# Alternating halves for negated weight sums, deferred follow-up work, and a gate in halves, in a one-layer hybrid decoder kernel

## The chip, the cores and the metric

The kernel runs on one core of a Trainium2 chip. The metric is the device time of one launch in microseconds (us); lower is better. Three runs of the kernel before gave a median of 2035.74 us.

## The reference

One layer on x of shape (512 positions, 2048), float32. The parts that matter here:

```python
h = rms_norm(x, norm1_w)
proj = h @ w_in                       # q | k | v | z | x,B,C | dt
q, k, v, z, xbc, dt_raw = split(proj)
attn = moba_attention(rms_norm(q), rms_norm(k), v)     # 8 heads x 128
xbc = silu(causal_dwconv(xbc))                         # width 4
y = ssd_chunked_scan(xs, softplus(dt_raw + dt_bias), -exp(a_log), bm, cm) + d_skip * xs
y = rms_norm per group of 512 (y * silu(z))            # 2 groups
x = x + concat(attn, ssm) @ w_out
h = rms_norm(x, norm2_w)
u_gate, u_val = split(causal_dwconv(h @ w_up))         # width 3
return x + (silu(u_gate) * u_val) @ w_down
```

## The kernel before, in words

Every product is computed from float32 operands that are split in two: `hi` (a rounded copy, made by ScalarE) and `lo` (the rest, made by VectorE), and takes three matmuls: hi by hi, hi by lo, lo by hi. TensorE (PE) is fed from such splits all the time.

**Phase one** (lines up to about 1215) is the input projection, attention, the state-space part and the output projection. The weights arrive in chunks (`raw`, three buffers) and are used in *pieces*. A piece is 12 matmuls of 512 columns, or for the 16 pieces of the `wz` weights (k and dt, first pair of heads) 24 of 264 columns. The main loop (line 1197) runs once for each piece `i`. It queues, in this order: the loads of chunks ahead; the matmuls of piece `i` (`use`), which at the last piece of a projection call `done`; the steps of `presum(i)`; the split of piece `i+3` (`issue_split`, which has three `hi` and three `lo` buffers, so that the split of piece `i+3` waits until the matmuls of piece `i` have read theirs); from the output projection on, splits of the mixed heads (`split_mix`); and one round of `advance()`.

Pieces 0 to 15 are the first x columns, 16 to 23 the B and C columns of group 0, 24 to 39 `wz`, 40 to 47 the queries of heads 0 and 1, 48 to 63 keys and values of the next pair, 64 to 71 their queries, 72 to 87 z of group 1, 88 to 111 x, B, C of group 1, 112 to 159 the two pairs of heads left, 160 to 175 z of group 0, and from 176 on the output projection. In the trace a query piece reads `acc<-A,hi`, a keys-and-values piece `acc<-hi,A`.

All other work of phase one is written as Python generators (`g_conv`, `g_q`, `g_head`, `g_ssm`, `g_gate` and so on). `spawn` runs the first step of one and puts it in a list; `advance` runs further steps when a rough clock for each engine (`Paced`) says that the step's inputs are ready, or at the latest in the second round for an urgent one (the step `"soon"` makes one urgent). Every engine works through its own queue in the order in which instructions were written, so that an instruction that waits holds all that are queued behind it. `done` of a query, of a convolution and of the last convolution call `spawn` at once, and so their first step is queued ahead of `presum` and the split of piece `i+3`.

- `g_conv`: VectorE scales the projection into `u`, ScalarE starts the tap sum `t`, VectorE adds three taps.
- `g_q`: ScalarE writes `qh`, VectorE `ql`, ScalarE the square `t`; the second step sums `t` over the head on PE (`token_sums`, line 636), and a copy of the sums goes to `rows`.
- `g_gate(g)`: four times a multiplication by the gate (VectorE) and a square into `sz` (ScalarE), three additions of the squares, sums on PE, a power of -1/2, a broadcast through PE into `p`, and four multiplications by it. Only then is `ssm0` or `ssm1` set, which `split_mix` of any tile of that group waits for (it forces generator steps until the name is there).

**Sums of weights ahead of time.** Phase two uses a scheme with seven products in place of eight, which needs sums of weight blocks. `presum` makes some of them in DRAM during phase one. For the `q`-th block of the list `SUMMED`, counted by `o = i - 6 * q`: at 12 a block is loaded into `s1t` (two buffers); at 15, for the first eight (`MINUS`), ScalarE writes its negative into `minus` (line 1182; in the trace `Y<-s1t`); at 16 and 18 GpSimd starts DMAs that add a further block into `s1t` and into `minus` (lines 1184, 1186); at 21 both are saved by DMAs on SyncE's queue (lines 1189, 1192; `s3d<-Y`). `minus` is the upper half of the tile `Y[1]` (4 x 512 elements in each partition), which holds nothing until group 1 begins. As 21 of block q is 15 of block q+1, the save of one block is queued just ahead of the write of the next, into the same half. The eight writes come in pieces 15, 21, 27, 33, 39, 45, 51 and 57.

**Phase two** (from line 1217) is the up and down projections; nothing in it is changed.

Of the kernel before, what the change touches and what calls it, by code (L numbers as in the profile page):

```python
# [195 lines left out]
def body(ctx, tc, xT, wi, wz, wo, wu, wd0, wd1, wd2, pp, pf, outT, dbg={}):  # L196
# [93 lines left out]
    C = [cpool.tile([128, S], F32R if k > 3 else F32, name=f"C{k}") for k in range(NH)] + [None] * 8  # L290
    first_v = C[4:8]
    Y = [cpool.tile([128, 4, S], F32, name="Y%d" % g) for g in range(2)]
    minus = Y[1][:, 2:4, :].rearrange("p a b -> p (a b)")
    for k in range(4, 8):
        C[k] = None

# [72 lines left out]
    st = {}  # L369


    gens = []

    def spawn(g, urgent=False):
        step([g, 0.0, urgent, 0, 1])
# [206 lines left out]
    def g_gate(g, sz):  # L582

        while "y%d" % g not in st:
            yield
        say = None if g else "ready"
        for f in range(4):
            clk["last"] = ("pe", clk["pe"])
            V.tensor_tensor(C[8 + 4 * g + f], C[8 + 4 * g + f], sz[:, f, :], op=OP.mult)
            A_.activation(sz[:, f, :], C[8 + 4 * g + f], AF.Square)  # L590
            if f % 2:
                yield say
        for f in range(1, 4):
            V.tensor_tensor(sz[:, 0, :], sz[:, 0, :], sz[:, f, :], op=OP.add)
        yield say
        p = sm_tile()
        token_sums(p, sz[:, 0, :])
        rows = wk.tile([128, 128], F32, name="rows", bufs=2)
        V.tensor_copy(rows, p[:, :128])
        yield say  # L600
        p = sm_tile()
        T.transpose(p[:, :128], rows, identf)
        r = wk.tile([128, 4], F32, name="scq", bufs=3)
        V.tensor_scalar(r, p[:, 0:128:32], 1.0 / 512, EPS, op0=OP.mult, op1=OP.add)
        G.tensor_tensor(r, r, nhalf[:, 0:4], op=OP.pow)
        yield say
        p = sm_tile()
        for t in range(4):
            T.transpose(p[:, t * 128:(t + 1) * 128], r[:, t:t + 1].to_broadcast([128, 128]), identf)
        for f in range(4):  # L610
            y = C[8 + 4 * g + f]
            V.scalar_tensor_tensor(y, y, pc("sw", 4 * g + f), p, op0=OP.mult, op1=OP.mult)
        st["ssm%d" % g] = True


    def g_q(acc, hd):
# [227 lines left out]
    def add_fm(done):  # L844
        box = {}
        for h in range(2):
            add_chunk(next_src("fm"), 1024, [512, 512], fm_uses(XR, 8 * h, [4, 4], NK, box, done))

    def conv_done(g, kind, ci, fi=0):
        def done(acc):  # L850
            if g not in sgs:
                while "y0" not in st:
                    advance(True)
                sgs[g] = ssm_group(g)
            spawn(g_conv(acc, ci, sgs[g], kind, fi), True)
        return done

    def wide(done, srcs, R, pre=None, tok=False):
# [40 lines left out]
    def z_stage(g):  # L899

        box = {}

        def done(t, acc):
            if t == 0:
                while not g and "ssm1" not in st:
                    advance(True)
                box["sz"] = wk.tile([128, 4, S], F32, name="sz")
            sz = box["sz"][:, t, :]
            clk["last"] = ("pe", clk["pe"])
            V.tensor_tensor(sz, acc, rbc, op=OP.mult)  # L910
            A_.activation(sz, sz, AF.Silu)
            if t == 3:
                spawn(g_gate(g, box["sz"]), False if g else "ready")

        wide(done, lambda k: next_src("wide"), XR)
# [23 lines left out]
    def add_pair(p):  # L939
        pr = {}  # L940
        hds = [{"i": 2 * p + i, "pair": pr} for i in range(2)]

        def kv_done(t, acc):
            if t == 0:
                while p == 2 and ("head2" not in st or "head3" not in st):
                    advance(True)
                pr["v"] = v_home(p)
                pr["k"] = wk.tile([128, 4, 256], F32, name="kt")
                pr["ss"] = wk.tile([128, 4, 2], F32, name="rk", bufs=2)
            vh, vl = (x[t] for x in pr["v"])  # L950
            A_.activation(vh, acc[:, 256:], AF.Copy, scale=rstd[:, t:t + 1])
            V.tensor_copy(pr["k"][:, t, :], acc[:, :256])
            V.scalar_tensor_tensor(vl, acc[:, 256:], rstd[:, t:t + 1], vh.bitcast(F32),
                                   op0=OP.mult, op1=OP.subtract)
            if t == 3:
                spawn(g_keys(pr))
                for hd in hds:
                    spawn(g_head(hd))

        def kz_done(half):  # L960
            def done(t, acc):
                if half == 0:
                    if t == 0:
                        pr["v"] = v_home(p)
                        pr["k"] = wk.tile([128, 4, 256], F32, name="kt")
                        pr["ss"] = wk.tile([128, 4, 2], F32, name="rk", bufs=2)
                    V.scalar_tensor_tensor(dtr[:, t, :], acc[:, 248:264], rstd[:, t:t + 1], pc("dtb", 0, 16),
                                           op0=OP.mult, op1=OP.add)
                    V.tensor_copy(pr["k"][:, t, :248], acc[:, :248])
                    if t == 3:  # L970
                        spawn(g_dt())
                    return
                vh, vl = (x[t] for x in pr["v"])
                A_.activation(vh, acc[:, 8:264], AF.Copy, scale=rstd[:, t:t + 1])
                V.tensor_copy(pr["k"][:, t, 248:], acc[:, :8])
                V.scalar_tensor_tensor(vl, acc[:, 8:264], rstd[:, t:t + 1], vh.bitcast(F32),
                                       op0=OP.mult, op1=OP.subtract)
                if t == 3:
                    spawn(g_ssm(0, sgs[0]))
                    spawn(g_keys(pr))  # L980
                    for hd in hds:
                        spawn(g_head(hd))
            return done

        if p == 0:
            for half in range(2):
                box = {}
                for k in range(0, NK, 2):
                    add_chunk(next_src("kz"), 528, [528], [tok_use(k, 2, 264, box, kz_done(half))])
        else:  # L990
            wide(kv_done, lambda k: next_src("wide"), XR, tok=True)
        for hd in hds:
            add_fm(lambda acc, hd=hd: spawn(g_q(acc, hd)))

    add_pair(0)
    add_pair(1)
# [2 lines left out]
        add_fm(conv_done(1, "xs", 4 + i, i))  # L999
    add_fm(conv_done(1, "Bf", 9))  # L1000
    last_conv = conv_done(1, "Cf", 11)
    add_fm(lambda acc: (last_conv(acc), spawn(g_ssm(1, sgs[1]))))
    add_pair(2)
    add_pair(3)
    z_stage(0)
# [2 lines left out]
    def split_mix(i):  # L1008

        k = OK_ORDER[i]  # L1010
        name = "ssm%d" % ((k - 8) // 4) if k >= 8 else "head%d" % k
        while name not in st:
            advance(True)
        dump("mix%d" % k, C[k])
        A_.activation(A[i], C[k], AF.Copy)
        V.tensor_tensor(B[i], C[k], A[i].bitcast(F32), op=OP.subtract)
# [156 lines left out]
    def presum(i):  # L1173
        for q, g in enumerate(SUMMED):
            w = blocks[g][2].shape[-1]
            o = i - 6 * q
            if o == 12:
                s1t[g] = wk.tile([128, 1024], F32, name="s1t", bufs=2)
                nc.sync.dma_start(s1t[g][:, :w], blocks[g][2])
            elif o == 15 and g in MINUS:  # L1180
                s3t[g] = minus
                nc.scalar.activation(s3t[g][:, :w], s1t[g][:, :w], AF.Copy, scale=-1.0)
            elif o == 16:
                nc.gpsimd.dma_start(s1t[g][:, :w], blocks[g][3], accum_op=OP.add)
            elif o == 18 and g in s3t:
                nc.gpsimd.dma_start(s3t[g][:, :w], blocks[g][0], accum_op=OP.add)
            elif o == 21:
                s1d[g] = dram.tile([128, w], F32, name="s1d%d" % g)
                nc.sync.dma_start(s1d[g], s1t.pop(g)[:, :w])
                if g in s3t:  # L1190
                    s3d[g] = dram.tile([128, w], F32, name="s3d%d" % g)
                    nc.sync.dma_start(s3d[g], s3t.pop(g)[:, :w])
# [4 lines left out]
    for i, (ci, o, w, use) in enumerate(pieces):  # L1197
        issue_dma(ci + 3)
        clk["pe"] = max(clk["pe"], ready.get(i, 0.0))
        use(*his.pop(i))  # L1200
        presum(i)
        issue_split(i + 3)
        for j in mix_at.get(i - out_start, ()):
            split_mix(j)
        left = n_piece - i
        if left <= 8:
            issue_dma(n_raw + (8 - left) // 2)
        if left == 5:
            early_split("P1", raws[n_raw])
        if left == 2:  # L1210
            early_sum()
        advance()
# [453 lines left out]
```

## Time and profile before

| | |
|---|---|
| median of 3 runs | 2035.74 us (2035.19 to 2037.06) |
| the profiled execution | 2035.49 us |
| span in its profile | 2033.8 us |
| PE busy | 2018.0 us |
| VectorE (DVE) busy | 1561.2 us |
| ScalarE (ACT) busy | 1011.3 us |
| phase one ends at about | 770 us |

How to read it: the profile shows one execution. The span runs from the first to the last recorded instruction; 1.7 us of the launch lie outside it. In the view in order of time a row has its start, its length, engine, line, operation, the tile written and the tiles read, and the number of instructions put together; in square brackets stand the time that the engine sat idle before it and what it was waiting for. "L191" is the helper through which phase one issues its operations. PE rows of length 0.39 overlap with the next matmul, which starts earlier than that. SPq is SyncE's queue of DMAs.

### The profile page before, as it was taken

What the parts mean: (1) busy time and instruction counts of PE and PEld (TensorE: products, weight loads), DVE (VectorE), ACT (ScalarE), POOL (GpSimd) and SP (SyncE); (2) the same over time, 40 slices, a digit from 0 to 9 for tenths busy, and PEclk for the clock granted to TensorE, in tenths of its full rate; (3) what the DMA queues carried; (4) which work ended last, traced back from release to release, by engine and by line L of the source; (5) the groups of instructions that cost most, each with busy time, mean ns of one, the idle gap of its engine ahead of it and who ended that gap; (6) DMA issues with size and microseconds to landing.
All of it is one profiled execution on the core that took longest, in us unless ns stands there. A gap on an engine that the chain in (4) does not pass through costs nothing.

```text
span 2033.8 us, 36927 instructions
## 1 busy us (share of the span) xinstructions
PE 2018.0 (99%) x14952; PEld 1887.6 (93%) x14952; DVE 1561.2 (77%) x2196; ACT 1011.3 (50%) x1476; POOL 201.7 (10%) x131
## 2 busy tenths in 40 slices
PE   9999999999999999999999999999999999999999
PEld 8887888878787889999999999999999999999999
DVE  6545654456556558999999999999999997967877
ACT  6534334333454446555555555555555664744643
POOL 0131000000000000101101101101110011001010
PEclk9999999999999999999999999999999999999999
DMA  6777655663224546445445445445444778867873
GB/s 213 213 208 197 181 145 180 189 190 109 80 80 138 181 156 238 163 147 189 164 146 190 162 147 191 162 146 194 159 146 155 258 220 250 252 172 221 241 239 125
DMA packets 126683, 362.92 MB, mean 178 GB/s; under 512 B 11952, under 2 KB 39984, under 8 KB 123696
## 3 DMA queue, kind: packets, MB, share of 16 engines
q1 hardware_dynamic: 119168, 335.64, 48.1%
q0 software_dynamic: 7056, 24.78, 6.9%
q8 instruction: 117, 1.92, 0.4%
q14 instruction: 54, 0.44, 0.1%
q10 hardware_dynamic: 288, 0.14, 0.0%
HBM read 303.69 MB, written 58.39 MB: 178 GB/s over the span
## 4 chain that ended last, share of the span: by engine, by line
PE 97%; DVE 1%; DMA 1%; ACT 1%; issue 0%; SPq 0%; ACTq 0%; DVEq 0%
PE acc L191 31%; PE x L1631 16%; PE x L1633 16%; PE x L1630 16%; PE sm L191 4%; PE y L1631 3%; PE y L1633 3%; PE y L1630 3%; PE x L1622 2%; PE x L1614 2%; PE sm L558 0%; PE y L1622 0%; DVE lo L191 0%; DMA raw<-wz 0%; DMA s3d<-Y 0%
## 5 line engine op out<-in xcount | busy, mean ns | idle before, releaser
L1630 PE MATMUL x<-cmb,hi 128*128 128x256 f32 x2922 | 681.9, 277 | 0.0
L1631 PE MATMUL x<-cmb,hi 128*128 128x256 f32 x2922 | 681.6, 276 | 0.0
L1631 PEld LDWEIGHTS x<-cmb,hi 128*128 128x128 f32 x2922 | 549.0, 188 | 0.0
L1630 PEld LDWEIGHTS x<-cmb,hi 128*128 128x128 f32 x2922 | 548.6, 188 | 0.0
L1633 PE MATMUL x<-cmb,lo 128*128 128x256 f32 x2922 | 392.8, 276 | 0.0
L1633 PEld LDWEIGHTS x<-cmb,lo 128*128 128x128 f32 x2922 | 359.4, 188 | 0.0
L191 DVE TENSOR_TENSOR lo<-raw,hi 128x512 fp32r<-128x512 f32 (+2 forms) x241 | 164.3, 688 | 230.9 <-ACT hi L191 216.1
L1317 DVE TENSOR_TENSOR lo<-rawa,hi 128x1024 fp32r<-128x1024 f32 (+1 forms) x225 | 270.0, 1200 | 13.7 <-PE x L1633 10.2
L191 PE MATMUL acc<-A,hi 128*128 128x512 f32 x704 | 279.4, 397 | 0.8 <-ACT hi L191 0.8
L191 PE MATMUL acc<-B,hi 128*128 128x512 f32 x704 | 275.5, 391 | 1.0 <-DVE B L191 1.0
L191 PE MATMUL acc<-A,lo 128*128 128x512 f32 x704 | 275.6, 392 | 0.0
L191 ACT ACTIVATE hi<-raw 128x512 fp32r<-128x512 f32 (+2 forms) x241 | 150.1, 627 | 241.0 <-PE acc L191 209.1
L1308 ACT ACTIVATE hi<-s 128x1024 fp32r<-128x1024 f32 (+1 forms) x179 | 179.0, 1001 | 171.8 <-DVE s L1285 100.0
L1308 ACT ACTIVATE hi<-rawa 128x1024 fp32r<-128x1024 f32 (+1 forms) x225 | 230.9, 1027 | 33.0 <-PE x L1631 20.0
L1317 DVE TENSOR_TENSOR lo<-s,hi 128x1024 fp32r<-128x1024 f32 (+1 forms) x179 | 213.0, 1190 | 29.3 <-issue 18.8
L1281 POOL TENSOR_TENSOR rawb<-rawa,rawb 128x1024 f32<-128x1024 f32 (+1 forms) x51 | 124.0, 2432 | 706.0 <-DVE s L1285 667.6
L191 PEld LDWEIGHTS acc<-A,hi 128*128 128x128 f32 x704 | 133.0, 189 | 29.2 <-issue 1.6
L191 PEld LDWEIGHTS acc<-A,lo 128*128 128x128 f32 x704 | 132.7, 189 | 28.8 <-DVE lo L191 0.8
L191 PEld LDWEIGHTS acc<-B,hi 128*128 128x128 f32 x704 | 133.0, 189 | 27.8 <-DVE B L191 1.7
L1477 ACT ACTIVATE cP<-x 128x256 f32<-128x256 f32 x132 | 50.5, 384 | 195.9 <-PE x L1633 195.9
L1630 PE MATMUL y<-cmb,hi 128*128 128x256 f32 x506 | 118.1, 277 | 0.0
L1631 PE MATMUL y<-cmb,hi 128*128 128x256 f32 x506 | 118.1, 276 | 0.0
(286 smaller groups left out, 2856.4 us busy)
## 6 DMA issues: line engine op xcount, KB each, us to landing
rawa<-wu SPq DMA_DIRECT2D x169, 512.0 KB, 3.8
raw<-wi SPq DMA_DIRECT2D x79, 512.0 KB, 3.7
rawa<-wd SPq DMA_DIRECT2D x54, 448.0 KB, 4.8
gd<-gt SPq DMA_DIRECT2D x22, 1024.0 KB, 4.4
rawb<-wu SPq DMA_DIRECT2D x40, 512.0 KB, 4.4
raw<-wo SPq DMA_DIRECT2D x32, 512.0 KB, 3.7
ld<-gd SPq DMA_DIRECT2D x27, 512.0 KB, 6.9
rawa<-wd SPq DMA_DIRECT2D x26, 512.0 KB, 5.0
```

The source lines that it names most:

```text
L191: return fn(out, *args, **kw)
L1281: (ve if gi in quick else po).tensor_tensor(r, raw[gi, "11"][:, :n], r, op=OP.subtract)
L1308: se.activation(h[:, :n], src[:, :n], AF.Copy)
L1317: ve.tensor_tensor(l[:, :n], src[:, :n], h[:, :n].bitcast(F32), op=OP.subtract)
L1477: se.activation(g[x], X[:, 256:] if x == "P5" else X[:, :256], AF.Copy)
L1614: pe.matmul(out, a[:, q * 128:(q + 1) * 128], b[:, q, :], start=False, stop=last and q == n - 1, skip_group_check=True)
L1622: pe.matmul(out, a[:, q * 128:(q + 1) * 128], b[:, q, :], start=fresh and q == 0 and a is h and not last, stop=last and q == n - 1, skip_g ...
L1630: pe.matmul(out, w, bk[:, 0, q, :], start=fresh and q == 0, stop=False, skip_group_check=True)
L1631: pe.matmul(out, w, bk[:, 1, q, :], start=False, stop=False, skip_group_check=True)
L1633: pe.matmul(out, l[:, q * 128:(q + 1) * 128], bk[:, 0, q, :], start=False, stop=q == n - 1, skip_group_check=True)
```

## The change

1. `minus` becomes two tiles, the lower and the upper half of `Y[1]`; block q uses the half `q % 2`.
2. The `spawn` of a convolution, of a query and of the scan of group 1 at the end of a projection is put in a list `ended`, and is called after `issue_split(i + 3)` of the same piece.
3. `g_gate` adds the squares in pairs as soon as each pair is made and adds the two results afterwards (three additions as before), and multiplies two of the four tiles by the scale, reports them, yields, and then does the other two. The names are `ssm00`, `ssm01`, `ssm10`, `ssm11`; `split_mix` waits for the half that it reads, and `z_stage(0)` for `ssm11`.

```diff
-    minus = Y[1][:, 2:4, :].rearrange("p a b -> p (a b)")
+    minus = [Y[1][:, i:i + 2, :].rearrange("p a b -> p (a b)") for i in (0, 2)]
...
+    ended = []
...
             if f % 2:
+                V.tensor_tensor(sz[:, f - 1, :], sz[:, f - 1, :], sz[:, f, :], op=OP.add)
                 yield say
-        for f in range(1, 4):
-            V.tensor_tensor(sz[:, 0, :], sz[:, 0, :], sz[:, f, :], op=OP.add)
+        V.tensor_tensor(sz[:, 0, :], sz[:, 0, :], sz[:, 2, :], op=OP.add)
...
         for f in range(4):
+            if f == 2:
+                st["ssm%d0" % g] = True
+                yield say
             y = C[8 + 4 * g + f]
             V.scalar_tensor_tensor(y, y, pc("sw", 4 * g + f), p, op0=OP.mult, op1=OP.mult)
-        st["ssm%d" % g] = True
+        st["ssm%d1" % g] = True
...
-            spawn(g_conv(acc, ci, sgs[g], kind, fi), True)
+            ended.append(lambda: spawn(g_conv(acc, ci, sgs[g], kind, fi), True))
...
-                while not g and "ssm1" not in st:
+                while not g and "ssm11" not in st:
...
-            add_fm(lambda acc, hd=hd: spawn(g_q(acc, hd)))
+            add_fm(lambda acc, hd=hd: ended.append(lambda: spawn(g_q(acc, hd))))
...
-    add_fm(lambda acc: (last_conv(acc), spawn(g_ssm(1, sgs[1]))))
+    add_fm(lambda acc: (last_conv(acc), ended.append(lambda: spawn(g_ssm(1, sgs[1])))))
...
-        name = "ssm%d" % ((k - 8) // 4) if k >= 8 else "head%d" % k
+        name = "ssm%d%d" % ((k - 8) // 4, k // 2 % 2) if k >= 8 else "head%d" % k
...
-                s3t[g] = minus
+                s3t[g] = minus[q % 2]
...
         issue_split(i + 3)
+        while ended:
+            ended.pop(0)()
```

## The prediction

> **What bounds the kernel now.** I read the page first, then busy time by stretches, then PE, ACT, DVE and SPq in order of time wherever PE sat idle.
>
> ```profile
> span 2033.8 us, 36927 instructions
> PE 2018.0 (99%) x14952; PEld 1887.6 (93%) x14952; DVE 1561.2 (77%) x2196; ACT 1011.3 (50%) x1476; POOL 201.7 (10%) x131
> ...
> 150.00:200.00 50.00, 45.78 (x232) 35.97 (x230) 26.98 (x63) 22.08 (x43) 7.38 (x8) 0.97 0.76 206
> 1000.00:2034.00 1034.00, 1030.25 (x9077) 1029.87 (x9075) 916.68 (x1096) 547.31 (x706) 115.37 (x60) 1.00 0.57 189
> ...
> 628.23 141.51 PE acc L191 x623
> ```
>
> The third and fourth rows are stretches: length, then busy time of PE, weight loads, DVE, ACT, POOL, then the granted clock. PE is the bound: 2018.0 of 2033.8 us, and phase two leaves only 3.75 us of 1034. So an edit of phase one is worth just what it changes in PE's waits. The last row, of the chain that ended last, gives the pace: 141.51 / 623 = 0.227 us for a matmul of 512 columns. A row's length is 0.39, so a wait costs its idle time plus the overlap of 0.16 that is lost. The worst stretch is 150 to 200 us, where both PE's busy time (45.78 of 50) and the clock (0.97) are down. There the first cause stands on ACT:
>
> ```profile
> 123.63 0.47 ACT L191 ACTIVATE C<-acc,rstd 128x256 fp32r<-128x256 f32 x1 [0.25 <-PE acc L191]
> 128.14 0.95 ACT L1182 ACTIVATE Y<-s1t 128x896 f32<-128x896 f32 x1 [4.04 <-DMA s3d<-Y]
> 152.88 0.95 ACT L1182 ACTIVATE Y<-s1t 128x896 f32<-128x896 f32 x1 [8.15 <-DMA s3d<-Y]
> ...
> 125.18 0.33 SPq L1192 DMA_DIRECT2D s3d<-Y  x1
> 147.30 0.38 SPq L1192 DMA_DIRECT2D s3d<-Y  x1
> ```
>
> Twice the negation stands at the head of ACT's queue for 4.04 and 8.15 us, because the save of the block before has just been issued (125.18, 147.30) and still reads the same half. Behind it wait the `hi` splits, and behind these DVE's `lo` and more. What PE pays:
>
> ```profile
> 129.66 0.50 PE L191 MATMUL acc<-A,hi 128*128 128x512 f32 x1 [0.60 <-ACT hi L191]
> 135.22 0.41 PE L191 MATMUL sm<-la,tri 128*128 128x32 f32 x2 [2.26 <-DVE la L191]
> 154.41 0.50 PE L191 MATMUL acc<-hi,A 128*128 128x512 f32 x1 [1.07 <-ACT hi L191]
> 155.13 0.50 PE L191 MATMUL acc<-lo,A 128*128 128x512 f32 x1 [0.22 <-DVE lo L191]
> 160.68 0.66 PE L636 MATMUL sm<-t,ones 128*32 128x128 f32 x8 [2.76 <-ACT t L191]
> ...
> 136.47 0.63 PE L191 MATMUL acc<-A,hi 128*128 128x512 f32 x1
> 136.90 0.63 PE L191 MATMUL acc<-B,hi 128*128 128x512 f32 x1
> ...
> 136.40:139.80 3.40, 3.40 (x9) 0.51 0.92 334
> 160.50:163.70 3.20, 3.02 (x14) 0.50 1.06 250
> 527.50:528.60 1.10, 0.07 (x2) 1.00 0.97 287
> ```
>
> The last three rows are stretches with PE's busy time and the clock alone. After each of the two longest idles (2.26 and 2.76 us) PE runs at half clock for about 3.4 us, with 0.43 us from one matmul to the next (136.47 to 136.90); around the 1.03 us idle at 527 the clock stays at 1.00.
>
> **The change part by part.** The sum starts from the profiled execution: 2033.8 of span and 1.7 around it, 2035.5, which is 0.25 below the median of the three runs.
>
> *Halves of the idle tile.* No instruction is added; the eight negations and sixteen DMAs stay. The save that a negation must wait for is now the one of two blocks before, queued six pieces (6 x 12 x 0.227 = 16 us) earlier, and landed. Whether the halves of one tile are told apart when waits are placed is shown by the gate, whose four tiles are slices of one:
>
> ```profile
> 515.32 1.28 DVE L191 TENSOR_TENSOR Y<-Y,sz 128x512 f32<-128x512 f32 x2
> 516.04 1.24 ACT L191 ACTIVATE sz<-Y 128x512 f32<-128x512 f32 x2 [1.36 <-DVE Y L191]
> ```
>
> The second multiplication writes its slice right behind the first, while ACT reads the first slice from 516.04: no wait on the whole tile. So the negation at 128.14 starts at 124.10, when the row at 123.63 ends. What is late next is its other input, the load of `s1t`, queued three pieces before: 8.2 us, against 4.5 typical and 10.3 at worst for that load:
>
> ```profile
> DMA to landing us min/median/max: 4.0/4.5/10.3
> ```
>
> An excess of 2.1 us would be covered by the two pieces (5.4 us) by which a split is ahead. Then, wait by wait:
> - 129.66: `hi` is ready 4 us earlier. Gone: 0.60 + 0.16 = 0.76.
> - 135.22: `la` ends a DVE chain that begins with the late `lo`, in the next rows; 5.5 us from 129.64 to 135.16. Begun at 125.7 it ends at 131.2; PE comes there at 128.9 + 12 x 0.227 = 131.6. Gone, with 0.4 to spare: 2.26 + 0.16 = 2.42.
>
> ```profile
> 129.64 0.69 DVE L191 TENSOR_TENSOR lo<-raw,hi 128x512 fp32r<-128x512 f32 x1 [4.95 <-ACT hi L191]
> 134.99 0.17 DVE L191 COPY la<-loga 128x32 f32<-128x32 f32 x1
> ```
>
> - Half clock after it: 8 matmuls x (0.43 - 0.227) = 1.6. Gone with the idle.
> - 154.41 and 155.13: the split is ready some 7 us before it is needed. Gone: 1.07 + 0.16 + 0.22 + 0.16, and 0.11 for the slow restart (0.50 in place of 0.39) = 1.7.
> - 160.68: the token sums of head 1 need `t`, at the end of this chain:
>
> ```profile
> 156.33 1.65 DVE L191 TENSOR_SCALAR E<-E,acs 128x128 f32<-128x128 f32 x8
> 158.01 0.63 ACT L191 ACTIVATE E<-E 128x512 f32<-128x512 f32 x1
> 158.54 0.67 ACT L191 ACTIVATE qh<-acc,par 128x512 fp32r<-128x512 f32 x1
> 160.03 0.60 ACT L191 ACTIVATE t<-acc 128x512 f32<-128x512 f32 x1 [0.82 <-DVE ql L191]
> ```
>
> It doesn't vanish. Counted from the end of piece 46: a split (0.6 `hi`, 0.7 `lo`), the eight subtractions (1.65), the last exponential (0.6), 3.55; now the split of piece 50 ahead of `qh` (0.55, part 2 of the change), then from `qh` to the end of `t` 2.1: 6.2. PE reaches the sums after pieces 47 and 48, 5.45. An idle of 0.75 stays; with the overlap 0.85 of the present 2.92, so 2.05 are gained.
> - Half clock after that: 3.02 us of work at 0.50 is 1.5 at full clock, so 1.5 are gained. An idle of 0.75 should bring no slow stretch (1.03 at 527 brought none).
>
> Sum of this part: 0.76 + 2.42 + 1.6 + 1.7 + 2.05 + 1.5 = 10.0.
>
> [...]
>
> *Splits ahead of what an ended projection sets off.* The gain is where a `lo` stands behind a convolution's taps:
>
> ```profile
> 78.93 2.33 DVE L191 SCALAR_TENSOR_TENSOR t<-u,par,t 128x512 f32<-128x512 f32 x3 [0.94 <-ACT t L191]
> 81.17 1.32 DVE L191 TENSOR_TENSOR lo<-raw,hi 128x528 fp32r<-128x528 f32 x2
> 81.93 0.39 PE L191 MATMUL acc<-lo,A 128*128 128x264 f32 x1 [1.58 <-DVE lo L191]
> ```
>
> The three taps of the C convolution (2.33) come first, and PE waits 1.58. With `lo` ahead it is done near 78, before PE wants it at 80.2: 1.6 gained. The taps then stand before the `lo` of the next piece, done near 82.4 and wanted at 83.0: covered with 0.6.
>
> The cost is on the queries: one `hi` (0.55) is now ahead of `qh`, and the sums on PE keep their place, one piece behind. Head 6:
>
> ```profile
> 522.63 0.60 ACT L191 ACTIVATE t<-acc 128x512 f32<-128x512 f32 x1 [0.82 <-DVE ql L191]
> 523.74 0.43 PE L636 MATMUL sm<-t,ones 128*32 128x128 f32 x8
> ```
>
> `t` ends at 523.23, PE is there at 523.74; 0.55 later it is 0.05 to 0.1 late. Heads 4 and 5 have the same distance, heads 0, 2, 3 and 7 more: 3 x 0.1 = 0.3 lost. The convolutions' own results are used several pieces later; their delay (a split, 1.3 us) costs nothing while the generators keep that distance, and up to a PE wait each if not. The deferral also shifts the rough clocks by a split, so a step may be queued a piece earlier or later. No row prices it: I bound it by the largest wait that a generator's step causes now, 2.9 (head 1) lost, and by 1.1 (the one at 527) gained, and take zero: nearest are the many steps without any wait.
>
> *The gate in halves.* The same three additions. Group 1:
>
> ```profile
> 526.19 2.14 DVE L191 TENSOR_TENSOR sz<-sz 128x512 f32<-128x512 f32 x3
> 528.25 0.28 DVE L191 COPY rows<-sm 128x128 f32<-128x128 f32 x1
> 528.59 0.33 PE L191 MATMUL sm<-identf,rows 128*128 128x128 f32 x1 [1.03 <-DVE rows L191]
> ```
>
> Two additions move from here to the squares, and `rows` comes 1.4 us earlier, ahead of PE: 1.1 gained (idle 1.03, little overlap behind short transposes). At their new place each waits for a square; the `lo` behind it is delayed by 0.2 or less, with pieces to spare. Group 0:
>
> ```profile
> 624.86 2.72 DVE L191 SCALAR_TENSOR_TENSOR Y<-Y,par,sm 128x512 f32<-128x512 f32 x4
> 627.50 0.68 DVE L191 TENSOR_TENSOR B<-Y,A 128x512 fp32r<-128x512 f32 x1
> 628.23 0.50 PE L191 MATMUL acc<-B,hi 128*128 128x512 f32 x1 [1.04 <-DVE B L191]
> ```
>
> With two multiplications in place of four ahead of it, `B` starts 1.35 us earlier, at 626.15, and ends at 626.8; PE wants it at 627.03. Gained: 1.04 + 0.16, say 1.15. The other two follow behind the next `lo` and `B`, and their results are wanted two pieces (5.4 us) later for 1.3 us of work.
>
> **Sum:** 10.0 + 1.6 - 0.3 + 1.1 + 1.15 = 13.55. 2035.5 - 13.55 = 2022.0.
>
> **Rivals.**
> - *The waits move.* ACT and DVE now have less time in 125 to 165 us, and a chain that hid behind the stalls, as `la` (0.4 to spare) or the exponentials, holds PE again for over 2 us, with half clock. Against it: the same generators run at full pace from 400 to 510 us for group 1. For it: head 1 is late by my own count already. Price: 2.05 and 1.5 not gained, and 0.85 more: 2022.0 + 4.4 = 2026.4.
> [...]
> - *The halves aren't told apart*, and the negation waits as before: only 1.6 - 0.3 + 1.1 + 1.15 = 3.55 is gained, 2032.0. Against it: the gate's rows.
> - *Slower: the query chain.* ACT is held up by more than the one split, and the sums of heads 2 to 6 wait as head 1's do now: 2.92 and 1.5 of half clock each, 5 x 4.4 = 22 lost against 10 gained (13.55 without the 3.55 at head 1): 2047.5. It decides if each waits over 2.0 us; the count gives 0.1.
>
> **How the numbers follow.** Forecast 0.65, its own range 2019.5 to 2025 (2.5 better: 1.1 for shifted steps, 0.85 at head 1 and 0.3 at the others not lost, and rounding; 3 worse: 2.9 for shifted steps); waits move 0.14, half clock stays 0.07, halves not told apart 0.06, slower 0.04, other partial losses 0.04. A measurement can tell 0.2%, 4 us, from no change; 2032.0 falls within that (0.2% below the median is 2031.7). So faster 0.88, same 0.07, slower 0.05. The range 2019 to 2028 takes in the first three cases, some 0.85.
>
> **What would show it.** Right: ACT's negations without a wait for `s3d`, no idle over 1 us on PE between 120 and 170 us, a clock of 1.00 there, a short wait (0.3 to 1.2) at head 1's token sums, none at 80, 527 and 626 us, and phase two as long as before. Wrong: an idle over 2 us anywhere in phase one, a negation that waits for `s3d` or long for `s1t`, token sums of heads 2 to 6 that wait over 0.3 us.

## The result, and the profile after

The changed kernel takes 2025.15 us (median of 4 runs, 2024.36 to 2025.43) against 2035.47 of the kernel before (4 runs): a ratio of 0.9948, 95% interval 0.9931 to 0.9965, so some 10 us or 0.5% faster. Forecast were 2022.0 and a gain of 13.55.

The page after, its first lines, and three stretches (the columns are those shown before):

```profile
span 2023.5 us, 36923 instructions
...
PE 2014.4 (100%) x14952; PEld 1885.4 (93%) x14952; DVE 1561.3 (77%) x2196; ACT 1011.2 (50%) x1476; POOL 201.8 (10%) x131
...
100.00:150.00 50.00, 50.00 (x324) 44.93 (x322) 26.17 (x70) 21.56 (x35) 18.96 (x9) 1.00 0.84 235
150.00:200.00 50.00, 49.17 (x275) 39.17 (x274) 28.23 (x59) 19.89 (x39) 5.41 (x6) 1.00 0.83 226
600.00:650.00 50.00, 47.67 (x219) 38.87 (x218) 29.16 (x55) 21.42 (x41) 1.01 (x1) 1.00 0.44 138
```

From 150 to 200 us PE is busy for 49.17 in place of 45.78 us, and the clock is 1.00 in place of 0.97. But between 600 and 650 us PE now loses 2.3 us, where it lost 1.0. The waits of PE (line, what it waited for, us in total, times, longest) say where:

```profile
PE sm L191 <- POOL scq L191: 2.3, 1, 2.3
PE acc L191 <- POOL nhalf L191: 1.0, 1, 1.0
PE sm L191 <- DVE P L191: 0.6, 3, 0.2
PE sm L640 <- ACT t L191: 0.6, 1, 0.6
PE acc L191 <- DVE lo L191: 0.4, 1, 0.4
...
```

The wait for `nhalf` is the start of the kernel, the same in every version. The waits for `la`, for `hi` and `lo` behind the negation, for `lo` at 80 us, for `B` and for `rows` are gone. The wait for `t` is down from 2.76 to 0.61. Two are new: GpSimd's power `scq` and a `lo`. In order of time, ACT's negations and the three waits of PE that are left or new:

```profile
123.32 0.94 ACT L1186 ACTIVATE Y<-s1t 128x896 f32<-128x896 f32 x1
...
138.75 0.94 ACT L1186 ACTIVATE Y<-s1t 128x896 f32<-128x896 f32 x1
```

```profile
72.15 0.50 PE L191 MATMUL acc<-A,lo 128*128 128x512 f32 x1 [0.41 <-DVE lo L191]
...
150.68 0.32 PE L640 MATMUL sm<-t,ones 128*32 128x128 f32 x4 [0.61 <-ACT t L191]
...
613.92 0.32 PE L191 MATMUL sm<-identf,scq 128*128 128x128 f32 x1 [2.33 <-POOL scq L191]
```

The negations have no idle time ahead of them, where they had 4.04 and 8.15 us.

The trace gives the start of every piece on PE, and the difference of after minus before at chosen pieces splits the gain (us; minus is earlier; every stretch left out is within 0.1):

| stretch of pieces | what is in it | forecast | measured |
|---|---|---|---|
| 0 to 12 | first loads | 0 | +0.7 |
| 20 to 24 | new wait at 72 us | 0 | +0.5 |
| 24 to 28 | wait at 80 us | -1.6 | -1.8 |
| 40 to 52 | negation, head 1, half clock | -10.0 | -10.7 |
| 120 to 152 | token sums of heads 4 and 5 | +0.2 | 0.0 |
| 156 to 160 | `rows` at 527 us | -1.1 | -1.2 |
| 160 to 192 | gate of group 0 | -1.15 | +1.6 |
| phase two | nothing changed | 0 | +0.7 |

Start-up and phase two differ as much among executions of kernels that are alike there: piece 12 begins at 38.6 to 39.9 us, and phase two takes 1264.2 to 1265.1 us, from its first matmul to the end of the span, in six profiles (before, after, and the first four experiments).

### The profile page after: what moved, and what is told of

The parts are those of the page before. It is cut to its first block, busy times and chain, and to the rows that moved or that the text cites. A ratio compares the mean times of both kernels' runs of the same rounds, so it can differ in the third digit from the quotient of the medians.

```text
span 2023.5 us, 36923 instructions
## 1 busy us (share of the span) xinstructions
PE 2014.4 (100%) x14952; PEld 1885.4 (93%) x14952; DVE 1561.3 (77%) x2196; ACT 1011.2 (50%) x1476; POOL 201.8 (10%) x131
## 3 DMA queue, kind: packets, MB, share of 16 engines
q8 instruction: 117, 1.92, 0.4%
## 4 chain that ended last, share of the span: by engine, by line
PE 98%; DVE 1%; ACT 0%; DMA 0%; issue 0%; POOL 0%; DVEq 0%; ACTq 0%; POOLq 0%
PE acc L191 31%; PE x L1636 16%; PE x L1637 16%; PE x L1639 16%; PE sm L191 4%; PE y L1637 3%; PE y L1636 3%; PE y L1639 3%; PE x L1628 2%; PE x L1620 2%; PE sm L559 0%; PE y L1628 0%; DMA raw<-wi 0%; DVE lo L191 0%; DVE t L191 0%; PE sm L640 0%
```

## The experiments

**Each part alone, and the suspected fault undone.** Two questions were open: which part carries the gain, and what makes PE wait for GpSimd at 612 us. My theory for the second: an addition that stands in the step of its squares makes the step's results due later by the rough clock, so the next step is queued a piece later. The rival: the deferral shifts the clocks. Beside the first four runs the kernel before took 2035.8 us (median of 21 runs).

*The halves alone.*

```diff
-    minus = Y[1][:, 2:4, :].rearrange("p a b -> p (a b)")
+    minus = [Y[1][:, i:i + 2, :].rearrange("p a b -> p (a b)") for i in (0, 2)]
...
-                s3t[g] = minus
+                s3t[g] = minus[q % 2]
```

> The kernel before with the two halves for the negated sums alone. Theory: the halves carry nearly all of the gain, since the negation no longer waits for the save of the block before: about 10.9 us faster than before, near 2024.6; the waits of PE at 129, 133, 153 and 158 us and both half-clock stretches are gone, the wait of 1.6 at 80 us and those of about 1.0 at 527 and 627 us stay. At head 1 (about 150 us) the token sums wait 0.0 to 0.2 us instead of 0.6, as no split stands ahead of the query. Rival: the gain comes from splits that no longer stand behind held work (part 2), and then this kernel gains under 2 us, 2033.5 or more.

Measured: 2025.07 us, ratio 0.9942 (0.9929 to 0.9954). ACT and the token sums of head 1:

```profile
124.50 0.94 ACT L1182 ACTIVATE Y<-s1t 128x896 f32<-128x896 f32 x1
139.92 0.94 ACT L1182 ACTIVATE Y<-s1t 128x896 f32<-128x896 f32 x1
...
151.31 0.43 PE L636 MATMUL sm<-t,ones 128*32 128x128 f32 x8
```

and PE's waits:

```profile
PE acc L191 <- DVE lo L191: 1.5, 1, 1.5
PE acc L191 <- DVE B L191: 1.0, 1, 1.0
PE acc L191 <- POOL nhalf L191: 1.0, 1, 1.0
PE sm L191 <- DVE rows L191: 1.0, 1, 1.0
...
```

No wait for the save, none at head 1, and those at 80, 527 and 627 us unchanged. By the starts of the pieces it gains 11.3 us between pieces 40 and 52 and nothing elsewhere (start-up was 0.4 longer and phase two 0.9). So this edit of two lines is worth as much as the whole change.

*The deferral alone* (all `ended.append(...)` of the change, nothing else).

> The kernel before with the deferred spawns alone. Theory: the wait at 80 us goes (1.8 gained), a new one of about 0.5 comes at 71 us, the negation still waits 4 and 8 us and PE's waits and half clocks of 128 to 164 us stay; 0.5 to 1.5 us faster, near 2034.5, too little to tell from no change. Rival (the deferral carries the gain): 5 us or more faster. Second rival for the new wait of the changed kernel at 612 us (GpSimd's power for the gate of group 0): if the deferral's shift of the rough clocks makes it, it appears here.

Measured: 2036.27 us, ratio 0.9996 (0.9987 to 1.0005), no difference; the expected 0.5 to 1.5 us did not show. The negation still waits:

```profile
130.19 0.95 ACT L1183 ACTIVATE Y<-s1t 128x896 f32<-128x896 f32 x1 [5.56 <-DMA s3d<-Y]
...
153.75 0.95 ACT L1183 ACTIVATE Y<-s1t 128x896 f32<-128x896 f32 x1 [8.02 <-DMA s3d<-Y]
```

1.8 us are gained at 80 us and 1.2 at 527. Lost are 0.5 at 72 us, 0.5 between pieces 28 and 40, 1.1 from piece 40 to 52, and 1.7 in start-up and phase two. The 1.1 is not shown to be the deferral's: the gate-alone kernel below defers nothing and loses 1.2 there too, and in both profiles the negation near 130 us waits longer for the save (5.56 and 5.34 us) than before (4.04). PE does not wait for `scq`: the deferral isn't the cause of that. One thing I did not expect: the wait of 1.2 us in all for `rows` at 527 us is gone with the deferral alone. DVE makes a `lo` while it would wait for `qh`, and so the three additions ahead of `rows` begin 4.0 us after piece 156 (522.53) in place of 5.3 (526.19 after 520.93):

```profile
523.22 0.69 DVE L191 TENSOR_TENSOR lo<-raw,hi 128x512 fp32r<-128x512 f32 x1 [0.82 <-ACT hi L191]
523.83 0.75 DVE L191 SCALAR_TENSOR_TENSOR ql<-acc,par,qh 128x512 fp32r<-128x512 f32 x1
...
526.56 2.13 DVE L191 TENSOR_TENSOR sz<-sz 128x512 f32<-128x512 f32 x3
```

*The gate alone* (the three edits of `g_gate` with the new names, nothing else).

> The kernel before with the gate in halves alone. Theory: each addition now stands in the same step as its squares, so the step's results are due later by the rough clock and the sums of group 0 are queued one piece later; the last two steps are then forced together, and PE waits about 2.3 us for GpSimd's power at about 623 us, while 1.2 at 527 and 1.2 to 1.3 at 627 us are gained: no change, 2035.5 within 0.7. Rival (the deferral makes that wait): no wait for the power here, 2.4 us faster, 2033.1.

Measured: 2038.48 us, ratio 1.0006 (0.9997 to 1.0015), no difference. The wait is there without the deferral, and half clock follows it, which I had not expected:

```profile
626.41 0.48 PE L191 MATMUL sm<-identf,scq 128*128 128x128 f32 x1 [2.33 <-POOL scq L191]
...
624.10:626.40 2.30, 0.00 (x0) 0.97 0.12 27
626.50:629.60 3.10, 3.10 (x10) 0.50 0.36 141
```

So in this profile the gate's part alone gains 1.2 at 527 us and loses 2.8 over pieces 160 to 192. There 4.1 go at the wait, of which about 1.5 is the half clock, and 1.3 come back at `B`. The runs of this kernel differ in how much half clock they had: the mean clock was 0.997 in three of the 11, the profiled one among them, and 0.998 in eight.

*The changed kernel with the additions of group 0 as before.*

```diff
             if f % 2:
-                V.tensor_tensor(sz[:, f - 1, :], sz[:, f - 1, :], sz[:, f, :], op=OP.add)
+                if g:
+                    V.tensor_tensor(sz[:, f - 1, :], sz[:, f - 1, :], sz[:, f, :], op=OP.add)
                 yield say
-        V.tensor_tensor(sz[:, 0, :], sz[:, 0, :], sz[:, 2, :], op=OP.add)
+        for f in ((2,) if g else (1, 2, 3)):
+            V.tensor_tensor(sz[:, 0, :], sz[:, 0, :], sz[:, f, :], op=OP.add)
```

> The changed kernel, but the three additions of group 0 stand together again just ahead of its sums, as before; group 1 and the scaling in halves stay. Theory: the sums of group 0 are queued one piece earlier, the wait for GpSimd's power (2.3 idle, 2.6 us in all) goes, and the wait for B stays gone: 2.6 us faster than the changed kernel, near 2022.5. Rival: the power is late whatever the order of the additions, 2025.1. The phase of the clock does not matter in either.

Measured: 2022.29 us, ratio 0.9930 (0.9917 to 0.9942), 2.9 below the median of the changed kernel. By the starts of the pieces, pieces 160 to 192 take 2.4 us less and every stretch ahead of them the same within 0.1; phase two, where nothing differs, gives another 0.7. PE's waits have no `scq` and no `B`:

```profile
PE acc L191 <- POOL nhalf L191: 1.0, 1, 1.0
PE sm L191 <- DVE P L191: 0.6, 3, 0.2
PE sm L642 <- ACT t L191: 0.6, 1, 0.6
PE acc L191 <- DVE lo L191: 0.4, 1, 0.4
PE acc L191 <- ACT hi L191: 0.4, 1, 0.4
```

DVE shows the shift. First the changed kernel, then this one; from the second pair of products to the scaling of the sums:

```profile
589.61 0.69 DVE L191 TENSOR_TENSOR lo<-raw,hi 128x512 fp32r<-128x512 f32 x1 [1.03 <-ACT hi L191]
...
590.82 1.28 DVE L191 TENSOR_TENSOR Y<-Y,sz 128x512 f32<-128x512 f32 x2
592.80 0.69 DVE L191 TENSOR_TENSOR sz<-sz 128x512 f32<-128x512 f32 x1 [0.70 <-ACT sz L191]
...
599.03 0.68 DVE L191 TENSOR_TENSOR sz<-sz 128x512 f32<-128x512 f32 x1
...
607.14 0.28 DVE L191 COPY rows<-sm 128x128 f32<-128x128 f32 x1
...
612.56 0.15 DVE L191 TENSOR_SCALAR scq<-sm 128x4 f32<-128x4 f32 x1
```

```profile
588.53 1.28 DVE L191 TENSOR_TENSOR Y<-Y,sz 128x512 f32<-128x512 f32 x2
...
596.39 2.14 DVE L191 TENSOR_TENSOR sz<-sz 128x512 f32<-128x512 f32 x3
...
604.49 0.28 DVE L191 COPY rows<-sm 128x128 f32<-128x128 f32 x1
...
609.92 0.15 DVE L191 TENSOR_SCALAR scq<-sm 128x4 f32<-128x4 f32 x1
```

With the addition in the first pair's step, everything from the second pair on is 2.3 to 2.7 us late, one piece. DVE's own time is not the reason: in the changed kernel it idles 1.03 us ahead of the `lo` behind which the second pair now stands, so the step was queued later. That the rough clock queued it later is read from the code (`Paced` adds the cost of each operation to its engine's clock) and was not followed value by value. The broadcast of the scale can't be later than just ahead of piece 187, because `split_mix` forces it there. So the transpose of `rows` and the broadcast, a piece apart before, stand side by side on PE, with DVE's scaling of the sums (612.56, behind a `lo`) and GpSimd's power (1.01 us) between them. Again the changed kernel first, whose broadcast is the row at 613.92 above, then this one:

```profile
611.32 0.27 PE L191 MATMUL sm<-identf,rows 128*128 128x128 f32 x1
612.86 1.01 POOL L191 TENSOR_TENSOR scq<-scq,nhalf 128x4 f32<-128x4 f32 x1 [61.84 <-DVE scq L191]
```

```profile
608.67 0.27 PE L191 MATMUL sm<-identf,rows 128*128 128x128 f32 x1
...
611.53 0.60 PE L191 MATMUL sm<-identf,scq 128*128 128x128 f32 x4
```

**What the deferral is worth, and a better version.** Both on one chip, beside the same runs of the kernel before (2035.16).

*No deferral*: the last kernel with all three `ended.append(...)` undone.

> Halves of the idle tile, additions of group 0 as before, additions of group 1 in pairs, scaling in halves; nothing deferred. Theory: the deferral gives 1.8 at 80 us and takes back 0.6 at 71 us and 0.7 at head 1, and so is worth about 0.5: this kernel is at most 0.5 slower than the one with it, near 2022.7, with a wait of about 1.6 at 80 us and none for head 1. Rival: the deferral also carries the gain at 527 us (the sums of the gate and of the head came in another order with it), then PE waits about 1 us for rows again and the time is 2024.

Measured: 2022.9 us, ratio 0.9939 (0.9927 to 0.9952). By the starts of the pieces it loses 1.3 against the last kernel (pieces 0 to 28) and gets 0.5 back at head 1 and 0.4 in pieces 160 to 192. The gain at 527 us stays, so the gate's additions in pairs suffice for it. The deferral as a whole is worth about half a microsecond, by the pieces; the times, 0.6 apart and from two chips, can't tell it.

*One convolution deferred.*

```diff
-            spawn(g_conv(acc, ci, sgs[g], kind, fi), True)
+            go = lambda: spawn(g_conv(acc, ci, sgs[g], kind, fi), True)
+            ended.append(go) if ci == 10 else go()
```

> As the kernel without deferral, but the one convolution at 74 us (C of group 0) is deferred. Theory: its taps no longer stand ahead of the split that PE wants at 80 us, and nothing else moves: 1.7 faster than without any deferral, near 2021, the fastest of all; no wait at 71, 80, 150, 527, 612 and 627 us. Rival: the wait moves to the next split, which has 0.6 to spare behind the same taps, and 1 us or less is gained.

Measured: 2021.0 us (2020.29 to 2021.09), ratio 0.9930 (0.9917 to 0.9944), 1.9 below the kernel without deferral: all five runs lie below all five of that kernel, and by the pieces 1.8 of it lies between 24 and 28. It is the lowest median of all, though its ratio equals that of the additions as before, 0.9930 on another chip. All the waits of PE that the view lists, the first two at the start of the kernel:

```profile
PE acc L191 <- POOL nhalf L191: 1.0, 1, 1.0
PE acc L191 <- ACT hi L191: 0.5, 1, 0.5
PE sm L191 <- DVE P L191: 0.4, 2, 0.2
```

**When does an idle PE lose half its clock?** The 2.33 us wait for `scq` brought half clock (0.50 behind it) in the gate-alone kernel and none (1.00) in the changed one, so the forecast's account of the clock was open. The probe adds 23 waits to the output projection of the kernel with the additions of group 0 as before.

```diff
+    pr = consts.tile([128, 64], F32, name="pr")
+
+    def probe(n):
+        p = sm_tile()
+        nc.tensor.transpose(p[:, :128], identf, identf)
+        nc.vector.tensor_copy(pr, p[:, :64])
+        for _ in range(n):
+            nc.vector.tensor_copy(pr, pr)
+        nc.tensor.transpose(p[:64, 128:256], pr, identf)
...
+        if i >= 194 and i % 2 == 0:
+            probe((1, 4, 6, 8, 10, 13)[(i // 2) % 6])
```

> The changed kernel with the additions of group 0 as before, and 23 extra waits of PE in the output projection (a small transpose, a chain of 2 to 14 copies on VectorE, a transpose of its result), two pieces apart; the result is unused. It measures when an idle brings half clock. Theory: the clock is decided on a fixed grid of 3.413 us, by how much of one grid interval PE idles, and the mark lies between 1.8 (no drop at the gate of group 0 in the changed kernel) and 2.2 us (drop at 133 us in the kernel before): an idle of 2.3 drops the clock only if it falls within one interval, one under 1.8 never, one over 4.4 always. Rival A: only the length counts, with a mark between 1.6 and 2.3: then idles over 2.3 always drop it. Rival B: a whole interval of 3.4 must be idle: then no idle under 3.4 drops it.

Measured: 2105.32 us in one run; the profile has waits of 0.55 to 4.36 us. Three of them, and the stretch behind each (length, PE busy, clock):

```profile
705.18 0.30 PE L1208 MATMUL sm<-identf,pr 128*64 128x128 f32 x1 [3.23 <-DVE pr L1207]
757.84 0.30 PE L1208 MATMUL sm<-identf,pr 128*64 128x128 f32 x1 [2.15 <-DVE pr L1207]
673.44 0.42 PE L1208 MATMUL sm<-identf,pr 128*64 128x128 f32 x1 [3.30 <-DVE pr L1207]
...
705.30:708.70 3.40, 3.40 (x16) 1.00 0.22 84
758.50:761.80 3.30, 3.30 (x9) 0.50 0.00 0
673.50:676.50 3.00, 3.00 (x8) 0.50 0.00 0
```

The idle of 3.23 us kept the full clock and the one of 2.15 lost it. The records of the clock begin and end on a grid of 3.413 us: in the profile of the kernel before they meet at 136.435, 139.848, 160.329, 163.742 and 2034.246 us, which are 1, 6, 1 and 548 steps apart. Divided by that grid, the 3.23 falls into 1.92 and 1.31, the 2.15 into one interval, the 3.30 into 3.00 and 0.29. I divided all idles over 0.3 us behind the first 10 us of six profiles so (before, after, the three parts alone, the probe). Every one of the 32 that leave at most 1.92 us idle in any one interval kept the clock, and all 19 with 2.12 us or more in one lost it for the next interval. One of the 19, of 4.36 us, which left a whole interval idle, lost it for two. Rival A (length alone) and rival B (a whole interval) both fall.

## Why the prediction was right, and where it was wrong

The signs named for a right forecast came: no negation waits, PE idles at most 0.61 us between 120 and 170 us at a clock of 1.00, and nothing is left at 80, 527 and 626 us. But one of the signs named for a wrong one came too, an idle over 2 us in phase one. The measured 2025.15 lies just above the forecast's own range (2019.5 to 2025). It is also what the forecast's case "half clock stays" (0.07) comes to, 2022.0 + 1.6 + 1.5 = 2025.1; only the trace, with a mean clock of 1.000, tells the two apart, so that number is a coincidence.

- *The halves.* Right, mechanism and size: 10.0 forecast, 10.7 measured in the whole change and 11.3 alone. `hi`, `la` and `lo` came in time, and the negation's next input, `s1t`, held nothing.
- *Head 1.* A wait of 0.75 was forecast, 0.61 came, and without the deferral none that the view lists: it is the one split ahead of the query, as put there. (In the sum, 0.75 and the overlap of 0.16 make 0.91 and not 0.85; that is 0.06 of the result.)
- *The half clock.* It went with the idles, so the 1.6 and 1.5 were rightly counted and the case in which it stays did not come. But the reading behind them, that it follows the longest idles (2.26 and 2.76 us, not 1.03), was incomplete: in the probe 3.23 us was free of it, and 2.15 was not.
- *80 us.* 1.6 forecast, 1.8 measured. Missed: the same deferral holds back the convolution before it too, the `lo` behind its taps comes 0.5 us later beside PE's pieces, and PE waits 0.41 at 72 us. I had followed the edit through the one projection where it helps, not the one before.
- *Queries.* 0.1 of loss was forecast at each of heads 4 to 6; at heads 4 and 5, which can be told apart, none came.
- *The gate, group 1.* Right: 1.1 forecast, 1.2 measured. The additions in pairs suffice for it without the deferral, but the deferral alone removes the same wait, which the forecast did not count.
- *The gate, group 0.* This step failed. `B` was on time, as forecast, but a wait of 2.33 for GpSimd came, which the text did not name. I priced the moved additions by the DVE time behind them, 0.2 us, "with pieces to spare", and took nothing for their effect on the rough clock. This chain had no piece to spare: it ends at a forced step. I named the deferral as what shifts the clocks, and it was the gate. The bound of 2.9 for shifted steps was large enough for this wait, but it was set for the deferral and taken from head 1; that it held is luck.

The 3.3 us that are short of the forecast are thus the wait for `scq` (2.6 with its overlap), 0.5 at 72 us, and 1.4 of start-up and phase two, which no edit touches, less 1.2 by which the other terms came out better.

## What to carry to other kernels

A scratch tile that is saved and rewritten at the same step of a loop can make its writer wait for the save, here at four of eight writes for 14.5 us in all; a second half is cheap, and what it is worth is read from what stands behind the waiting instruction in its queue. Where a planner places steps by estimated times, an operation added to a step also moves every later step: count, for a chain that ends at a forced step, how many steps are left until then. Putting the splits ahead everywhere gained hardly more than it lost; at the one place where the trace showed PE waiting behind it, it gained 1.9 us.

## What the runs showed of the hardware

In the six profiles divided above, PE's clock fell to half for the next interval of the grid of 3.413 us after each of the 19 idles that took 2.12 us or more of one interval, and after none of the 32 that took at most 1.92. So the same wait cost by its place: 2.33 us cost 2.6 in the changed kernel (1.75 and 0.58 in two intervals) and about 4.1 in the gate-alone kernel (2.17 in one). The kernel before, with idles of 2.26 and 2.76 us, ran between 2033.41 and 2040.02 us, the fastest version between 2020.29 and 2021.09. A part of the spread of the kernel before goes with its mean clock: of its 21 runs, the ten with a mean clock of 0.999 took 2033.41 to 2037.36 us and the five with 0.997 took 2038.75 to 2040.02. As an estimate from the grid, one interval at half clock is 3.413 / 2 = 1.7 us of 2035, or 0.0008 of the mean clock, so these are one interval against three or four. Which idles dropped the clock in those runs was not traced.
